# Another table of queue orders for a two-layer diffusion trunk on one Trainium2 core

## The chip, the cores and the metric

The kernel runs on one core of one Trainium2 chip. A core has five instruction queues that run side by side and meet only at semaphores: TensorE (PE, the matmuls; their weight loads are shown apart as PEld), VectorE (DVE), ScalarE (ACT), GpSimd (POOL) and SyncE (SP, which issues most loads). The metric is the device time of one execution in microseconds (us); lower is better.

## What is computed

A diffusion trunk of two layers over 512 latent tokens and 256 context tokens of width 1024, in float32. Every sub-layer stands between two RMS norms, with shift, scale and gate worked out from a conditioning vector (adaLN). Layer 0 mixes tokens by neighbourhood attention beside spatial gating, layer 1 by retention; each is followed by a gated MLP with a depthwise convolution of three taps. Cut to what matters:

```python
def conv_ffn(h, w_in, conv_w, conv_b, w_out):
    a = dwconv3(h @ w_in, conv_w, conv_b)
    gate, up = jnp.split(a, 2, axis=-1)
    return (jax.nn.silu(gate) * up) @ w_out

for i in range(2):
    sh1, sc1, g1, sh2, sc2, g2 = jnp.split(silu(c) @ ada_w[i] + ada_b[i], 6, axis=-1)
    h = modulate(rmsnorm(x, norm_g[i, 0]), sh1, sc1)
    y = hybrid_na_sgu(...) if i == 0 else retention_mixer(...)
    x = x + g1 * rmsnorm(y, norm_g[i, 1])
    h = modulate(rmsnorm(x, norm_g[i, 2]), sh2, sc2)
    x = x + g2 * rmsnorm(conv_ffn(h, ...), norm_g[i, 3])
```

In layer 0 the context tokens go through the same steps, with a conditioning vector of their own.

## The kernel before

**Matmuls.** Tokens are cut into six tiles of 128 rows (t = 0 to 3 latent, 4 and 5 context). A float32 product is made of three fp32r matmuls: each operand x is split into a rounded copy hi (ACT, L171) and the rest lo = x - hi (DVE, L172), and `mm3` issues hi by hi, hi by lo and lo by hi (L216 to L218), all into one PSUM tile. PSUM has three groups of tiles, A (four buffers), B and C (two each). A PE instruction that opens a new PSUM tile waits until the tile before it in that buffer was read out by ACT or DVE.

**The FFN.** The products of the tokens with the two halves of w_in (gate and up) use a two-level Strassen-like scheme: sums of weight blocks (the split tiles wa, wb, wc and wd, built by DVE at L1618 to L1630 and split at L171 and L172) times sums of token blocks (blk, hb, hs; in layer 0 they travel through DRAM on their way, L607 and L622). The results px and py (L215 to L218) are emptied into the tile pre by ACT (L1574) and DVE (L1579); convolution (ACT L1586, DVE L1587 and L1590), Silu (L1593) and product (L1594) give g. In layer 1 the first blocks are made by plain products, pf, with the weights wp. The product with w_out, tile wf, is copied by ACT (L1730) into one of four slots (yp0 twice, ypg twice) and from there added to the rows yd or yf by a DMA with accumulation that POOL issues (L1734).

**Between sub-layers.** The last out-projection of the retention adds its PSUM tiles wrA and wrC to the token tiles yr (DVE L678); then come the square sums (ACT L403), the RMS factors (POOL L408 and L389), gate (DVE L434), residual (DVE L441), a second norm (L453 on DVE for one half of the row, L454 on ACT for the other), transposes on PE (tile ht, L552) and their scaling (ACT L560, DVE L562). In the attention the scores s (L1066, L1067) use keys ka and kb; kb is completed by a cast on POOL (L1021), and the bias tiles tm are made on POOL too (L1049 to L1056); softmaxed rows sc are transposed to pt (L1136) and multiplied with the values (L1144 to L1151). Beside all this runs the adaLN of later sub-layers: DVE accumulates weight rows (L326), PE sums them and turns them by two-column transposes (at, L370) or multiplies them out (ag, L347), and POOL loads the norm gains ngr (L352) and stores the gates (L356).

**What sets the order.** The program text records its instructions first. `Trunk.queue()` then reads the table ORDER: for each of the five engines it gives, as differences, a permutation of the instructions that were recorded for that engine, and `queue()` chains them with dependencies that need no semaphore, so that each engine issues its instructions in the order of the table. What an instruction waits for (data, free buffers) follows from the tiles and is the same in any order.

Of the kernel before, what the change touches and what calls it, by code (L numbers as in the profile page):

```python
# [51 lines left out]
c-p;Nd8{4RS^wtDnSI~x+<kxd?Yp1-{1(SsV#izD_}N+P#Ez4YCUKi4X_Is#ZBx`#Ep3Bn)0P4)sBEQz3Mx<wv>*_mB2>|Tsf0u&{s0Li{@`D}Gt  # L52
0d*cX6Ie%CYaAJ2Pj_obxTe@ArK(PX+)BbckC8n$bRh-#=2s?*@MGjDZ{0)zEWi_4p&YxNS9|21<GeE+yMdm<kKg;1FHHn!XWj=Hk6ia<||U96SM
gxYLERfTJ7&IFfcwwyOXOU;~&_5D$0i9{3c8+s|=Hk3Z)=&Xp_pLvwKOD!l9C9CZ5Er(4@Nyawbd{;D0^#BUOh4HuzeorTj$U$$VJ3^)O9%~&$Y^
gXs$hPS_|L;JJrYh^;`yOQmM^SCNW9Q?+14X)#N6+eglLBE61YPGFbfBsdF$BbhR9n7t}kjjg-dHg&EkH$N9N6SGWUKlfGyVIYPv63!T!*4Nj-{F
h0^JqlNc&nDZ;x!Il=d#i}GSvAIfCuv$Xk{&SzipDXu1`4rKWtK8CAnkg4*o)Rsx;no6MM+EEr1tcbD}YAvF(XeX7@v&$ZUr6R4qD!>ph2?U+18J
oBE^h?c}z-ak`$vB|Q9&PqQv3mYD&$*Wq*>fawyZ``woEv$%$z$0HPo&TJgIy{;Zb3sPgTFSB(y41P{#JEHS5aELB=Z}vnav-s}pg0oO(mKLA80q
|Y!J6!ILpC|FO5O*R$9ecKaYBR5RCZvzDi$4G#W`eqf=vRf8Q33#al-=|V4l#%!%0tN|XP9#&R&@D=;l=Jns9HoYdkWwtJb8QLm6O@vc9AJ(*d!0
+_I^7usKHWk>G0od_dhszlPwu%59|Nf@9-s(S@aX>O0oSu+kS%^Bb58|CcO?{WW9cceQ5~MQDdHr-hVU^-=zpPN1gVavHjuLPJ9`=3mf9uxAf_ZS
YSDsAHa4Tt|9@)&~!HO%IdM$Vg7-G&kp>}Pe%DZ2mi_?qg5m4u_~z-e33KZZ#npD4!)OmVVAx1RJ8cv`LH|7O!u|-JRcn#Mb)Fn;vwcL^RZ(?iS0  # L60
+T(zOV7!W@zhd)M|jxR350iLo`)2k0;xS%Pu6nrUvV1j8LYHIJ&SL^3^*&;)(#5ZR-+!d=+f&I8m--%L$vXTmJ*hT||XrVZMkaPW7@P|v_;2X^|k
{?A|Ih6gwoeLpZ^_?g6#(uVBet}k<MaJv)wA5B;Z{Cq-VATmBtijaCSodQk>H*8wB(kq`FiWLVMj8LtypHF9DV$h12aIijz#Wlu~97wc0A78N%Ay
cC5Z2Wz4oYr2Cr20lywx8qP|1YuZ{yr<h!^4+e0cOZ{Y+6zRc+j_=6a9JTA?x^dN~3bqDGp*Cz<0Rsa&&O+tGHV#{^?*g-{w|NXRghvt(*BB1t-Y
%Je8fvUvQB}=Q>=^=;q!1qfd|3MgGQFgN~P2h`ZXE6P3t$661kM?!1zjecY-!C-W0%v#zvawJ>t?{Cnb98`G!t!8q~vdAv|vg55M`WR^jm%_=|n@
xc+92E!h{njJqY_ow>%Spl7nY_s3$>6P0P986E$a&gE@6PS&^;t5Pe8*5lrXoE*CcSn?WJ*Gc-hLy={4&+F-h1xm?_hs$>J$ZZ4IvGJ^CA6De$v|
2|G^id6a4K`?*dVT~rBV0!0W-cZLM+9Rdv8QtkHSNK#@af=CQLxsSsm+;ebAlBT4Mo@9^R}(1b@JxUrx4bactPhs`>DhN%5u{OFp8tTiX{Oixa|W
M%#LD{6u`uhd<9H`5qqJVo1M`hO1a_>F!xJ`Ga}kB|usl{LY%v-gfMpAA(n53NQW)-sxAlMBeE@sYIIb3@-J<2peo+ae(8y{iK0~zMT;i8ujU&fu
_d7*CVmwx2wsxD<i2`qdpGxo*jp(N0O{8vhnxcJt0pT3A9Bf-}9sCNNly8388;{qr-{aI$k8u?CdYxo2EH#YNfStxZ6n~)J$Q$bs8du0^3`5R-}<
Oi>2YD^44P`K_MRh=Gk1z@xW**bSq0TGHN-4aP%qe!Hj%beI~TCIF!1pG&Q6Rrkm9vF>XYxsmokGVhs;;V?%#GytF|_;Oz3=1c^U4;2gI}R8LLlv
!CQQvCV~q3%ijnk0mBq>4(35W<Q;?)VFBj1S{Q*>Hc);mSal<Lny~i)3{6(nH0VGxVhhXkjbaM&;4a=3wxLG>yNpZYyW^_>C=<XuoExl`agZ=RfG  # L70
d$6!nKWZu?0x_Hd?saPrM=41T_E?9n^ZmXkvQb0~G+cS*(1B_Fwh#1IU=_(Ggtj%!``=^D+kma{Q!g#l<%0al)eBcC3K`-8(M+L=FhG5YbFaVM4}
{{en}Z$w2g2hA)isZ_<_`bu0Q8m%FuH00SkTG>a)N69{*`p&9r`)S1lp5yjv;w=4kK4sx|u1Xpe9^`$fGJ&Ap5D!}ze<gAW#yw7aA)V*rkd`+yEv
}b*gd605%1^i-bMTD2UuYSf`T8r&6?@q@)X5cnCyD1y6`S?)sQv*rQw;eUdE!p>d%=ii;6&OylVc4(3r!w97L&w8OoQ8P)shV04GvG;GwE(u2}<>
KF4Ea843$xNVn0j$Bd(vD-+=HomX@vDEW=wCOnyY*hh#Y6UV)!&D`ps0K8Z!xyXRD5g7>{$@T#Vn2B>>!z4Ssf`aP#$Br_gq@5j#zgN(yMc#LAj(
{XSqkV?PoJW3&wlKFrLPgKdnnKI37qV)P$x>Wh8pA9{e55<^^#I@A{>R-P708b+hy~Yh=>wWN3f@^Awjy?YT%{bEsCa_1c6a1a%_Rq!|{jCY4<VX
GEf5pL<xW%Xn3#`<dOlP*Ami`$x-f4co-3iXc-w*BY68rz)Qy+v^3UA$O*i3ekz?jKQSXdd99WWrAwo)c|=IqJa@X`;%M9y$q_O=)C2|e9C&hnqV
w^~SC`DCTuTmk7V+K=OY|HS13(6t;<j^ge6e!@MUsm1N9O^AeFkMH(nu3sfM2>+k$0*wuDDK@c}B6H7|5cUVL_ndm0_*wOiZF`bqJqvG(ihfp6E-
`cIw&`4c6?=p7b|#l`DsaFU;N!-DJBWNqYc+>XGGezmTpa989%v{uu_$<NU!rs4>WFFE%=zsPxxPYKq?r`)o{FB-jSt6}YEGXiXQ6Es@+IIAB0H$
QUws%Ce_#o$*SI0oJ)A?yZ*j@<Nr30Cvd2K*<<gs0``&bYNIv-^S>yXSUcK=#{Q3l!E5+@^N$XA~4gW?K-1Po)HuK)B<2?a`$L?bwJ`u@G?s@)KI
QEQsj+LwSAdcYye1=PLyp_{yCyl;?h%QGjP|!SX+<bg_nAG87zs-#}Mla7f^Vnm>b>4Sndv1<NM$BQn%2M9q$CA7L4VTM0?j8ladvb*HFpOuxQ|Y  # L80
3vWh+@9<GwXM{B%oM_hVll80=q4$wqUe$cS1v38!o)|Bxsep*(P@d52^SYHHwP)9J`hM1=ZuzpA)5NPN%atueOJ|H>@m>tx7)5&^2(uvL$?42Hzv
`I+SjmFY>1dB=zM0o&J;sUePhlpB=C;6KxytE2QFX7MYvwB+&J;M8x#N4^<V(vT{?6tkL@R1CA31>~Hok*E5R<iFm(=`VBeCda<z^ZCRl70bz3u_
WQ(?@nvL&B$oZoQ-J_!<onNmf28pdCST8=&+cwY0U#e$ai)`jPWwh4LKAm=Kg!OTC|dY?H3q<9v8t7R=kngUi5y*_qY|jzj8v1MYYQ;ovAwZ>dUW
lNvieo1QW?(%F4SY1l-|Aq7TC5VS7yBYh@pmn@k)Ha*?C|#z0b-Kb{}GGc=hkwoJ@X{w?nP&(Y?0xsfaOV0gAG`G++(;^$o~${x>xNwR=PpNv5|G
s1~sv6Q}&z3*$>ZEG|yPoQ{}zQirKG1U(!{WdU;`K*ovoJpoAmwiTY<18}<hSq(kyca%{1?{U@idl=%aA$&nygYJb^vV44SW1AHo=v3|Cl$$W*Sg
93X{Qt84%6u7^b<@soA7n^U8kmTEts&UsHy~XYG!uLk=muT!xWF0f_(fE6@1H-KJ-XSl?)e%KCPk!-+0Uh@5WWB0E(t+s$DB6IL47(q^IH>T@;kf
# [1959 lines left out]
```

## Time and profile before

| | |
| --- | --- |
| time, median of 3 runs | 1784.99 us (1783.62 to 1786.71) |
| time of the profiled execution | 1783.88 us |
| span of the profile | 1782.1 us |
| mean TensorE clock granted | 0.996 |
| HBM read, written | 191.80 MB, 39.85 MB |
| attention (layer 0) | about 190 to 345 us of the span |
| FFN of layer 0 | about 400 to 1040 us |
| FFN of layer 1 | from about 1418 us |

The span is the part of the execution between the first and the last recorded instruction; 1.8 us of the profiled time lie around it. A queue runs in order: an instruction that waits holds up all that stand behind it on its engine, and idle time of an engine costs only where the engine that ends last waits for it.

### The profile page before, as it was taken

What the parts mean: (1) busy time and instruction counts of PE and PEld (TensorE: products, weight loads), DVE (VectorE), ACT (ScalarE), POOL (GpSimd) and SP (SyncE); (2) the same over time, 40 slices, a digit from 0 to 9 for tenths busy, and PEclk for the clock granted to TensorE, in tenths of its full rate; (3) what the DMA queues carried; (4) which work ended last, traced back from release to release, by engine and by line L of the source; (5) the groups of instructions that cost most, each with busy time, mean ns of one, the idle gap of its engine ahead of it and who ended that gap; (6) DMA issues with size and microseconds to landing.
All of it is one profiled execution on the core that took longest, in us unless ns stands there. A gap on an engine that the chain in (4) does not pass through costs nothing.

```text
span 1782.1 us, 28774 instructions
## 1 busy us (share of the span) xinstructions
PE 1746.4 (98%) x11024; PEld 1576.8 (88%) x11024; DVE 1388.4 (78%) x2363; ACT 1017.1 (57%) x1882; POOL 338.9 (19%) x462
## 2 busy tenths in 40 slices
...
GB/s 306 116 133 168 96 109 43 107 180 119 171 178 172 180 172 153 169 172 160 271 112 135 109 120 64 119 98 86 90 72 60 107 126 152 206 220 183 177 148 129
DMA packets 84398, 253.44 MB, mean 142 GB/s; under 512 B 11026, under 2 KB 11538, under 8 KB 84260
## 3 DMA queue, kind: packets, MB, share of 16 engines
...
q14 instruction: 52, 0.43, 0.1%
HBM read 191.80 MB, written 39.85 MB: 130 GB/s over the span
## 4 chain that ended last, share of the span: by engine, by line
PE 89%; DVE 5%; ACT 2%; DMA 1%; issue 1%; POOL 1%; SPq 0%; DVEq 0%; POOLq 0%; ACTq 0%
PE px L215 12%; PE wf L216 5%; PE wf L217 5%; PE wf L218 5%; PE rn L217 4%; PE rn L216 4%; PE rn L218 4%; PE py L215 4%; PE px L218 2%; PE px L216 2%; PE px L217 2%; PE py L218 1%; PE py L217 1%; PE py L216 1%; PE ug L216 1%; PE ug L217 1%
## 5 line engine op out<-in xcount | busy, mean ns | idle before, releaser
L326 DVE SCALAR_TENSOR_TENSOR acc<-ar,cs,acc 128x512 f32<-128x512 f32 x256 | 190.1, 757 | 12.0 <-DMA ar<-in_adaw 5.1
L216 PE MATMUL rn<-rwv,h0c 128*128 128x256 f32 x384 | 107.8, 281 | 0.0
L217 PE MATMUL rn<-rwv,h0c 128*128 128x256 f32 x384 | 107.5, 281 | 0.0
L218 PE MATMUL rn<-rwv,h1c 128*128 128x256 f32 x384 | 107.2, 280 | 0.0
L1734 POOL DMA_DIRECT2D yf<-yp x64 | 55.9, 962 | 265.8 <-ACT yp L1730 238.3
L1574 ACT ACTIVATE pre<-px 128x256 f32<-128x256 f32 (+2 forms) x160 | 55.9, 369 | 78.2 <-PE px L215 56.1
L1587 DVE SCALAR_TENSOR_TENSOR cv<-pre,cw,cv 128x769 f32<-128x769 f32 (+1 forms) x88 | 77.2, 882 | 27.7 <-ACT cv L1586 27.1
L1586 ACT ACTIVATE cv<-pre,cw 128x770 f32<-128x770 f32 (+1 forms) x88 | 80.9, 925 | 21.5 <-DVE g L172 11.6
L1730 ACT COPY yp<-wf 128x512 f32<-128x512 f32 x118 | 68.3, 583 | 42.3 <-PE wf L218 34.4
L215 PE MATMUL px<-blk,wb 128*128 128x384 f32 (+1 forms) x480 | 78.8, 308 | 1.1 <-ACT pre L1574 1.1
L215 PE MATMUL px<-hs,wc 128*128 128x384 f32 (+1 forms) x480 | 78.7, 309 | 1.1 <-ACT pre L1574 0.8
L1590 DVE SCALAR_TENSOR_TENSOR cv<-pre,cw,cv 128x769 f32<-128x769 f32 (+1 forms) x88 | 76.8, 881 | 0.9
L215 PEld LDWEIGHTS px<-hs,wc 128*128 128x128 f32 x480 | 73.2, 188 | 4.2 <-ACT pre L1574 1.6
L215 PEld LDWEIGHTS px<-blk,wb 128*128 128x128 f32 x480 | 72.4, 188 | 3.8 <-ACT pre L1574 1.6
L171 ACT ACTIVATE wc<-q 128x512 fp32r<-128x512 f32 x80 | 49.8, 629 | 43.8 <-PE py L215 21.7
L216 PEld LDWEIGHTS rn<-rwv,h0c 128*128 128x128 f32 x384 | 72.4, 189 | 1.2 <-issue 0.2
L218 PEld LDWEIGHTS rn<-rwv,h1c 128*128 128x128 f32 x384 | 72.5, 189 | 0.7
L217 PEld LDWEIGHTS rn<-rwv,h0c 128*128 128x128 f32 x384 | 72.3, 188 | 0.9
L218 PE MATMUL rn<-rwg,h1c 128*128 128x256 f32 x256 | 71.3, 279 | 0.0
L1734 POOL DMA_DIRECT2D yd<-ypg x48 | 48.3, 1052 | 120.3 <-ACT ypg L1730 102.9
L217 PE MATMUL rn<-rwg,h0c 128*128 128x256 f32 x256 | 71.2, 279 | 0.0
L216 PE MATMUL rn<-rwg,h0c 128*128 128x256 f32 x256 | 71.1, 279 | 0.0
...
## 6 DMA issues: line engine op xcount, KB each, us to landing
...
```

The costliest lines, as they stand in the source:

```text
L171: self.S.activation(hi, src, AF.Copy)
L215: mm = lambda *p, **k: self.T.matmul(*p, skip_group_check=True, **k)
L216: mm(out, lhs[0], rhs[0], start=first, stop=False)
L217: mm(out, lhs[0], rhs[1], start=False, stop=False)
L218: mm(out, lhs[1], rhs[0], start=False, stop=last)
L326: V.scalar_tensor_tensor(out=acc[s], in0=raw[:, kk * 512 : kk * 512 + 512], scalar=self.cs[:, 8 * s + k : 8 * s + k + 1], in1=acc[s], op0= ...
L1574: S.activation(pre[:, i, c : c + w], ps[:, b : b + w], AF.Copy, scale=scale)
L1586: S.activation(d, s, AF.Identity, scale=w1, bias=b)
L1587: V.scalar_tensor_tensor(out=d[:, 1:W], in0=s[:, 0 : W - 1], scalar=w0, in1=d[:, 1:W], op0=ALU.mult, op1=ALU.add)
L1590: V.scalar_tensor_tensor(out=d[:, 0 : W - 1], in0=s[:, 1:W], scalar=w2, in1=d[:, 0 : W - 1], op0=ALU.mult, op1=ALU.add)
L1730: S.copy(v, ps)
L1734: G.dma_start((yd[t] if first else y[t])[:, o], v, accum_op=ALU.add)
```

## The change

Only the string ORDER differs: 72 lines of text become 112. No instruction is added or taken away, tiles and their buffers are the same; one more load of an activation table appears at the start, where ACT's order changes between two functions. The text of the table is compressed, so a line of it tells nothing by itself:

```diff
 LANES = ("PE", "DVE", "Activation", "Pool", "SP")
 ORDER = """
-c-p;Nd8{4RS^wtDnSI~x+<kxd?Yp1-{1(SsV#izD_}N+P#Ez4YCUKi4X_Is#ZBx`#Ep3Bn)0P4)sBEQz3Mx<wv>*_mB2>|Tsf0u&{s0Li{@`D}Gt
...
+c-pmlXLRJ)b>@8l3aJ1TfI{V*t4J1E%sDi3X0w}Qv%AR-(|M-jO!tHilQjyXFr#Eiqd2mHNA_wYTN+zFYiVuo`gqqX$79L)*p`pit6ke`uXoQ```CLgs>
...
```

The table being 40 lines longer, every line number behind it is 40 higher in the new kernel (L216 becomes L256, L1730 becomes L1770).

What it does is seen in the queues. PE's queue is printed with equal neighbours joined: it has 8847 rows before and 9761 now. ACT, in the FFN of layer 0, at block 9 (wc9 and wb9 are its weight sums, yp0 and ypg the slots for w_out's pieces wf). Before:

```order
L1730 COPY ypg_4613<-wf0430_5768 128x512
L1730 COPY ypg_4613<-wf0431_5815 128x512
L1574 ACTIVATE pre00_4125<-px08_5722 128x384
L171 ACTIVATE wc9_5856<-q49_5858 128x512
L171 ACTIVATE wb9_5806<-s29_5807 128x512
L1730 COPY yp0_4612<-wf0641_5874 128x512
L1730 COPY yp0_4612<-wf0640_5865 128x512
L171 ACTIVATE wb9_5806<-s39_5808 128x512
L1586 ACTIVATE cv08_5913<-pre00_4125,cw0_4123 128x770
```

and now:

```order
L1770 COPY ypg_4613<-wf0430_5768 128x512
L1614 ACTIVATE pre00_4125<-px08_5722 128x384
L211 ACTIVATE fo07h_5824<-fo07r_5826 128x1024
L1770 COPY ypg_4613<-wf0431_5815 128x512
L211 ACTIVATE wb9_5806<-s39_5808 128x512
L211 ACTIVATE wb9_5806<-s29_5807 128x512
L1770 COPY yp0_4612<-wf0640_5865 128x512
L1770 COPY yp0_4612<-wf0641_5874 128x512
L1626 ACTIVATE cv08_5913<-pre00_4125,cw0_4123 128x770
```

The copies of wf0640 and wf0641 stood behind the first split of wc9; now they stand ahead of both, which follow four and eleven rows behind.

POOL, some 30 us later in the same FFN (ngr0110 is a load of norm gains for a later sub-layer, yd0 the accumulating stores of token tile 0). Before:

```order
L1734 DMA yd5_4132<-ypg_4613 128x512 x2
L352 DMA ngr0110_6139<-in_norm_g 128x512
L1734 DMA yd0_4127<-yp0_4612 128x512 x2
L317 MEMSET acc100_6209 128x512
L317 MEMSET acc101_6212 128x512
L356 DMA g20_4110<-ngr0110_6139 128x512
```

and now:

```order
L1774 DMA yd5_4132<-ypg_4613 128x512 x2
L1774 DMA yd0_4127<-yp0_4612 128x512 x2
L392 DMA ngr0110_6139<-in_norm_g 128x512
L357 MEMSET acc100_6209 128x512
L392 DMA ngr0111_6205<-in_norm_g 128x512
L1774 DMA yd1_4128<-ypg_4613 128x512
L358 DMA acc100_6209<-in_adab_row 1x16x32
```

The two stores to yd0 have moved ahead of the load; the load ngr0111, which came nine rows after them, now comes ahead of the first store to yd1.

PE, at the end of the retention's out-projection and the start of the FFN of layer 1 (ht12 are the transposes of token tile 2, ht11 and ht10 those of tiles 1 and 0). Before, behind the last matmul of wrC21 stand three transposes, all twelve matmuls of wrC30, one transpose, all of wrC31 and then:

```order
L216 MATMUL wrC31_14642<-rwo71_14460,gt7_14438 128x512
L217 MATMUL wrC31_14642<-rwo71_14460,gt7_14438 128x512
L218 MATMUL wrC31_14642<-rwo71_14460,gt7_14438 128x512
L552 MATMUL ht110_14664<-ident_95,yr01_9944 128x128 x4
L552 MATMUL ht101_14602<-ident_95,yr00_9927 128x128 x4
L552 MATMUL ht111_14673<-ident_95,yr01_9944 128x128 x4
L552 MATMUL ht120_14774<-ident_95,yr02_9961 128x128 x4
L216 MATMUL pf100_14749<-hb1_14475,wp001_14463 128x256
```

Now the last matmul of wrC21 stands in the middle of wrC30:

```order
L258 MATMUL wrC30_14611<-rwo61_14324,gt16_13905 128x512
L256 MATMUL wrC30_14611<-rwo70_14455,gt7_14438 128x512
L592 MATMUL ht100_14593<-ident_95,yr00_9927 128x128
L258 MATMUL wrC21_14571<-rwo71_14460,gt7_14438 128x512
L257 MATMUL wrC30_14611<-rwo70_14455,gt7_14438 128x512
L258 MATMUL wrC30_14611<-rwo70_14455,gt7_14438 128x512
```

and 20 rows behind it:

```order
L258 MATMUL wrC31_14642<-rwo70_14455,gt7_14438 128x512
L256 MATMUL wrC31_14642<-rwo71_14460,gt7_14438 128x512
L592 MATMUL ht110_14664<-ident_95,yr01_9944 128x128
L257 MATMUL wrC31_14642<-rwo71_14460,gt7_14438 128x512
L258 MATMUL wrC31_14642<-rwo71_14460,gt7_14438 128x512
L256 MATMUL pf100_14749<-hb1_14475,wp001_14463 128x256
L256 MATMUL pf110_14790<-hb1_14475,wp101_14692 128x256
L592 MATMUL ht121_14785<-ident_95,yr02_9961 128x128
L592 MATMUL ht120_14774<-ident_95,yr02_9961 128x128
L592 MATMUL ht121_14785<-ident_95,yr02_9961 128x128
```

wrC20, wrC21, wrC30 and wrC31 are woven together, and the transposes of tiles 0 and 1 have moved in among them; ht12 follows right behind.

More of the change, by code (lines that the diff above doesn't have):

```diff
@@ L57 @@
[L57 to L71, printed above, removed]
```

169 lines of the change are left out of this document (112 added, 57 removed).

## The prediction

> **What bounds the kernel.** I read the busy shares first, then the chain of waits that ended last.
>
> ```profile
> span 1782.1 us, 28774 instructions
> PE 1746.4 (98%) x11024; PEld 1576.8 (88%) x11024; DVE 1388.4 (78%) x2363; ACT 1017.1 (57%) x1882; POOL 338.9 (19%) x462
> PE 89%; DVE 5%; ACT 2%; DMA 1%; issue 1%; POOL 1%; SPq 0%; DVEq 0%; POOLq 0%; ACTq 0%
> ```
>
> TensorE (PE) is the bound. The change issues the same matmuls, so it can only touch three things: the time PE waits, the time PE runs at half clock, and what it costs to go from one kind of matmul to another. The view of PE's waits (line, tile, who released it; sum, count, longest) prices the first:
>
> ```profile
> PE ht L1831 <- DVE xn L425: 9.7, 2, 8.0
> PE ht L552 <- ACT sa L560: 3.0, 1, 3.0
> PE wf L216 <- ACT yp L1730: 3.0, 2, 1.7
> PE px L215 <- ACT pre L1574: 1.9, 3, 0.8
> PE pt L1136 <- DVE at L172: 1.4, 3, 0.9
> PE s L1067 <- POOL kb L1021: 1.2, 1, 1.2
> PE wf L216 <- ACT pre L1574: 1.0, 1, 1.0
> PE s L1066 <- DVE sst L1123: 0.9, 1, 0.9
> PE py L215 <- ACT pre L1574: 0.5, 1, 0.5
> ...
> PE rq L216 <- ACT h0c L171: 0.2, 1, 0.2
> ```
>
> The eight largest rows sum to 22.1 us. The next twelve, from the 0.5 to the 0.2 shown, add 3.6. Of these 25.7 us, 9.7 are the start of the kernel, where PE has no data; 16.0 us are left for an order to win. The table by stretches (span, then busy us and count of PE, its weight loads, DVE, ACT and POOL, then clock, DMA share and GB/s) shows where the clock fell:
>
> ```profile
> 190.00:345.00 155.00, 150.20 (x1032) 124.51 (x1031) 122.13 (x344) 105.33 (x262) 36.91 (x51) 1.00 0.26 80
> ...
> 1405.00:1425.00 20.00, 16.18 (x82) 13.32 (x81) 18.09 (x34) 16.52 (x41) 7.62 (x14) 0.95 0.43 159
> 1425.00:1440.00 15.00, 14.62 (x108) 14.32 (x107) 13.99 (x26) 11.50 (x24) 2.15 (x2) 0.84 0.62 216
> 1440.00:1455.00 15.00, 14.40 (x120) 14.00 (x119) 13.26 (x21) 11.51 (x23) 0.00 (x0) 1.00 0.11 37
> 1455.00:1540.00 85.00, 83.28 (x591) 77.46 (x592) 82.50 (x130) 59.32 (x108) 10.41 (x12) 1.00 0.60 162
> ```
>
> At the start of layer 1's FFN the clock averages 0.95 over 20 us and 0.84 over 15 us: 1.0 + 2.4 = 3.4 us lost at most. DVE is the second fact in these rows: from 1405 to 1540 it is busy 18.09 + 13.99 + 13.26 + 82.50 = 127.8 of 135 us. Whatever the order, that stretch cannot shrink by more than about 7 us. The ceiling of the whole change is thus 16.0 + 3.4 us of waits and clock, and about 2 us of kinds of matmul (below): 21 us, 1.2%.
>
> **Places where the new order takes a wait away.** The largest clear one is the w_out product of layer 0's FFN, whose outputs (wf) ACT copies from PSUM to yp. The timeline (start, duration, engine, idle before and its releaser):
>
> ```profile
> 560.48 0.63 ACT L171 ACTIVATE wc<-q 128x512 fp32r<-128x512 f32 x1 [7.82 <-PE py L215]
> ...
> 561.53 1.05 ACT L1730 COPY yp<-wf 128x512 f32<-128x512 f32 x2
> 562.15 0.50 PE L216 MATMUL wf<-fo06h,g 128*128 128x512 f32 x1 [1.71 <-ACT yp L1730]
> ```
>
> ACT's queue stood 7.82 us on the split of wc9, whose buffer PE's py products still read, and the copies that free PSUM stood behind it. In the new order both copies stand ahead of both wc9 splits. PE has matmuls of the next products to run while they copy, so the 1.71 us go; nothing is newly late, since wc9 feeds products of the block after. The second is at 591 us:
>
> ```profile
> 584.73 0.57 POOL L352 DMA_DIRECT2D ngr<-in_norm_g  x1 [12.52 <-DVE wc L172]
> 585.29 1.78 POOL L1734 DMA_DIRECT2D yd<-yp  x2
> 590.93 0.58 ACT L1730 COPY yp<-wf 128x512 f32<-128x512 f32 x1 [2.17 <-DMA yd<-yp]
> 591.57 0.51 PE L216 MATMUL wf<-fo06h,g 128*128 128x512 f32 x1 [1.25 <-ACT yp L1730]
> ```
>
> POOL waited 12.52 us with the load of ngr0110 and kept two yd stores behind it; the yp copy waited for the store to land, and PE for the copy. The new order has the stores first. Behind the load now stand a memset, ngr0111 and the store of yd1, which is not due before the next pair of copies. Gain 1.25 us, and with the first place **-3.0**.
>
> The rows "px <- pre", "wf <- pre" and "py <- pre" (1.9 + 1.0 + 0.5 = 3.4 us) are PE waiting for ACT to empty px: at the starts of the two FFNs and once after the change of product group at 850 us. The new order interleaves the products of two outputs, so that each px has other matmuls behind its last one. I count cover (queued PE work between producer and consumer) that meets the copies at 850 us and at the start of FFN 0, and misses about a third of them after 1440 us, where DVE is at 13.26 of 15 us. Bounds 0 and -3.4; I take **-2.4**.
>
> In attention the rows pt, s and s (1.4 + 1.2 + 0.9 = 3.5 us) are round trips through ACT, DVE and POOL. The POOL cast of kb12 (L1021) now follows tm5 and not tm6, and PE has some four matmuls more ahead of kb12's first use; other scores lose cover. Adding up the missing cover in both orders I get about 4.5 us before and 3.2 now: **-1.3**, between 0 and -2.5.
>
> **A place where it looks worse: the start of FFN 1.** Token tile 2's last out-projection (wrC21) must pass residual, norms and a rescale before its transposes ht12:
>
> ```profile
> 1410.46 0.39 PE L218 MATMUL wrC<-rwo,gt 128*128 128x512 f32 x1
> ...
> 1413.55 0.39 PE L218 MATMUL wrC<-rwo,gt 128*128 128x512 f32 x1
> ...
> 1414.12 0.39 PE L217 MATMUL wrC<-rwo,gt 128*128 128x512 f32 x1
> ...
> 1416.43 0.39 PE L218 MATMUL wrC<-rwo,gt 128*128 128x512 f32 x1
> 1416.66 1.47 PE L552 MATMUL ht<-ident,yr 128*128 128x128 f32 x12
> 1421.17 0.63 PE L552 MATMUL ht<-ident,yr 128*128 128x128 f32 x4 [3.04 <-ACT sa L560]
> ```
>
> From the end of wrC21 (0.23 us after 1410.46, the spacing that 1416.43 and 1416.66 show) to ht12 went 10.5 us. Before, PE had 24 wrC matmuls (0.23 each) and 16 transposes (twelve take 1.47 us and four 0.63, so 0.84 / 8 = 0.105 each) to run: 7.2 us, and it waited 3.04. Now wrC20 to wrC31 are woven together, and behind wrC21's last matmul stand 15 wrC, 10 transposes and two pf of half the width: 4.7 us. If the chain still needs 10.5 us, the wait is 5.8, 2.8 more. But DVE, which sets the chain here (18.09 of 20 us), reaches wp101 after some 2 us less work in the new order, so later waits for it shrink: between -1 and +2.8, I take **+1.0**. I leave the drop of the clock as it is, since it followed a wait of this length and the wait grows.
>
> The Trainium skill, page "TensorE: Matmul & The Clock Gate", section "Why this matters for your kernels", asks for no PE idle gap above about 3 us, as one idle window brings the clock back to half. The trace agrees: 3.04 us of wait, then 0.84. By that rule an order which broke this wait into pieces under 3 us would win the 3.4 us as well, and the sum below would be -8.8; the new order does not break it.
>
> **Kinds of matmul.** Two-column transposes (at, L370) cost extra when they stand among wide products:
>
> ```profile
> 168.86 0.39 PE L218 MATMUL pk<-h0a,wk 128*128 128x512 f32 x1
> 169.18 0.40 PE L370 MATMUL at<-ident,arow 2*128 2x2 f32 x4
> 169.51 0.50 PE L216 MATMUL pv<-h0a,wv 128*128 128x512 f32 x1
> 169.84 0.39 PE L217 MATMUL pv<-h1a,wv 128*128 128x512 f32 x1
> ```
>
> ```profile
> L370 PE MATMUL at<-ident,arow x48: 195/197/219, 169.2 to 1348.4; 2*128 2x2 f32 x48
> ```
>
> From 168.86 to 169.84 are 0.98 us, of which the two wide matmuls are 0.46; the burst of four took 0.52. One lasts 0.197 (the median of 48, second fence) and four last 0.40, so a step is 0.068 and four are 0.27; the other 0.25 are the burst's entry and exit. The order has 19 such bursts before and 15 now: 4 x 0.25 = -1.0. The plain fp32 bursts fall by about three; their entry is at most the same 0.25 (0 to -0.75; I take -0.4). Together **-1.4**. The 128-column transposes are spread over twice as many bursts, at no price: from 1413.55 to 1414.12 stand two wrC (0.46) and between them one transpose alone, which so costs 0.11 us, as one of twelve in a row does.
>
> **The start.** ACT now squares xn04 first and loads the table for Silu after it; SP sends ident ahead of xn05.
>
> ```profile
> 0.72 1.28 ACT L223 ACT_TABLE_LOAD   x1 [0.72 <-PEq L2034]
> 6.69 0.63 ACT L403 ACTIVATE jx<-xn 128x512 bf16<-128x512 f32 x1 [0.62 <-DMA xn<-in_x]
> 10.14 0.90 PE L1831 MATMUL ht<-ident,xn 128*128 128x128 f32 x3 [1.67 <-DVE xn L425]
> 10.97 1.87 PE L266 MATMUL ad<-ar,cs 128*2 128x256 f32 x4
> ```
>
> A second table load of 1.28 us plus Silu less the 0.62 us that ACT idled puts xn05 some 0.75 us later. In exchange a transpose and two ad matmuls (1.87 / 4 = 0.47 each), 1.05 us, stand in PE's wait of 1.67. Bounds -1.05 and +0.75: **-0.3**. The last seventy rows of every queue are as before: 0.
>
> **What the tight order costs.** Counting, for each PE wait, how much queued work covers it, I find 94 covered by less than 0.5 us before and 220 now. The twelve small rows of the waits (3.6 us) over those 94 make 0.04 us each; 126 more make 0 to +4.8. Most of the new ones have more than 0.25 us of cover, so **+2.0**.
>
> The sum is -3.0 - 2.4 - 1.3 + 1.0 - 1.4 - 0.3 + 2.0 = -5.4 us on the profiled run of 1783.88 us (span 1782.1): 1778.5. The profiled run lies 1.1 us under the median of the three runs shown, 1784.99; half of that added, I forecast **1779.0**, 0.3% faster.
>
> **Rivals.** (a) Nearly every wait goes, that at FFN 1 too: 16.0 + 3.4 + 1.4 = 20.8 at most, 12 or more if DVE's 127.8 us in 135 let it: 1764 to 1772. For it speaks that all named waits are touched; against it ht12's cover of 4.7 for 10.5 us. Chance 0.12. (b) The waits change their places: the gain of -7.4 without the last term is eaten by new ones of 4 to 11 us: 1781 to 1788, no change. For it speaks the count 94 to 220. Chance 0.24. (c) Slower: a round trip across engines that the queue covers by under 0.25 us (50 before, 97 now) runs late by its hops. Above, PE started 0.1 us after the yp copy and store after copy cost more. At 0.12 us on each of the 97, 11.6 us, the gain is gone and 0.2% with it; at 0.15, 14.6 us, the time is 1792. Against it: the 50 of before cost at most the 3.6 us of small rows, 0.07 each. Chance 0.12. (d) The half clock comes more often: each drop is worth 3.4 us as at 1405, and three turn the sum to +4.8, 1789. Against it: attention lost 4.8 of 155 us in short waits at a clock of 1.00. Chance 0.04. The same page of the Trainium skill, in "A second HAM failure mode: psum-queue depth-cycling", tells of this: frequent short idles at PSUM buffers made the clock swing; the row of attention speaks against it here. That the table does nothing can be excluded: every queue differs from it by the order of rows.
>
> **Chances and range.** My forecast, between -3.6 and -12 us, has 0.48. Faster still is (a), 0.12; no change is (b); the slower side is (c) and (d), 0.16. A change under 0.2%, 3.6 us, can hardly be told from none here. Faster 0.60, same 0.24, slower 0.16. The range from 1766 to 1791 takes in the bounds of the terms (-3.4, -2.5, +2.8, +4.8) and most of (a) and (b).
>
> **What would show it.** Right: no 1.7 us row for wf, a POOL queue whose yd stores come before ngr, px rows under 1.5 us together, ht12 waiting 3 to 5 us with the clock at half after it, and some 4 to 6 us of waits of 0.1 to 0.4 us. Wrong: a stretch outside 1405 to 1455 below a clock of 1.00, a new wait above 2 us, or no wait at ht12.

## The result, and the profile after

The changed kernel takes **1775.99 us** (median of 5 runs, 1775.4 to 1776.8), against 1784.99 before: the ratio is 0.995, with a 95% interval of 0.9936 to 0.9965. The forecast was 1779.0, in a range of 1766 to 1791. The profiled execution took 1775.40 us, with a span of 1773.6; before they were 1783.88 and 1782.1, so 8.5 us went. The page's head and the shares of the chain that ended last:

```profile
span 1773.6 us, 28862 instructions
PE 1747.3 (99%) x11024; PEld 1570.8 (89%) x11024; DVE 1394.7 (79%) x2363; ACT 1025.0 (58%) x1883; POOL 344.5 (19%) x462
PE 47%; DVE 1%; POOL 1%; ACT 1%; issue 0%; DVEq 0%; POOLq 0%; ACTq 0%
```

PE's busy time is the same within 1 us, with the same 11024 matmul rows. The span shrank, so what went is time in which PE stood: span less busy time was 35.7 us before and is 26.3 now. (The chain's shares cannot be compared with those of before: the listed ones sum to 50% here and to 99% before.) PE's waits of the changed kernel (line, tile, releaser; sum, count, longest; the lines lie 40 further down, since the table is longer):

```profile
PE ht L1871 <- DVE xn L465: 7.8, 1, 7.8
PE pf L256 <- ACT hb L211: 2.6, 1, 2.6
PE pf L256 <- ACT wp L211: 1.3, 1, 1.3
PE rkc L258 <- DVE rwk L212: 0.7, 1, 0.7
PE px L255 <- ACT pre L1614: 0.6, 2, 0.4
...
PE py L255 <- ACT pre L1614: 0.4, 1, 0.4
PE pf L258 <- DVE wp L212: 0.4, 1, 0.4
PE rn L258 <- DVE h1c L212: 0.4, 1, 0.4
...
PE htc L527 <- DVE hc L538: 0.3, 1, 0.3
PE pt L1176 <- DVE sst L1163: 0.3, 1, 0.3
```

Of the rows of before, both for "wf <- yp" (3.0 us) and the one for "wf <- pre" (1.0) are gone, px and py wait 1.0 instead of 2.4, the second wait for xn is gone, and the three rows for pt and s in attention (3.5) have shrunk to one of 0.3 for pt. New are the row of 2.6 for pf, in place of 3.0 for ht at the same spot, 1.3 behind it, three at the start of the retention (rkc, rn, htc), and four of 0.3 to 0.5 us that are left out above; two of these, of 0.4 and 0.3 us, lie in attention. By stretches (span, then busy us and count of PE, weight loads, DVE, ACT and POOL; clock, DMA share, GB/s):

```profile
190.00:345.00 155.00, 153.64 (x1045) 127.68 (x1045) 125.81 (x349) 107.11 (x266) 37.97 (x53) 1.00 0.27 80
1415.00:1430.00 15.00, 12.92 (x86) 11.93 (x87) 13.78 (x26) 13.64 (x29) 4.71 (x6) 0.77 0.56 179
1430.00:1445.00 15.00, 15.00 (x129) 15.00 (x129) 15.00 (x25) 9.43 (x18) 0.00 (x0) 1.00 0.03 7
```

```profile
1415.35:1422.10 6.75, 5.02 (x19) 4.03 (x20) 5.53 (x10) 5.67 (x13) 4.10 (x6) 0.50 0.22 86
```

In attention PE is busy 153.64 of the same 155 us, 150.20 before, so it stands for 1.36 us and not for 4.80. At the start of FFN 1 the clock falls again, to 0.77 over 15 us; the last row shows that it is at half from the end of the wait of 2.55 us on, for 6.8 us.

To see **where** the time went I use rows of PE's queue ahead of which the very same matmuls stand in both orders, and take the difference of the times at which PE reaches them. Between two such rows the work is equal, so a change of the difference belongs to that stretch:

| stretch of the profile before, us | forecast for what lies in it | measured |
| --- | --- | --- |
| start, to 86 | -0.3 | -1.6 |
| 86 to 215, products ahead of attention | part of the tight order | +0.6 |
| 215 to 337, attention | -1.3 | -3.05 |
| 337 to 410, start of FFN 0 | part of -2.4 (px, wf, py <- pre) | -1.0 |
| 410 to 598, the two places with yp and yd | -3.0 | -3.05 |
| 598 to 857, change of product group | part of -2.4 | -0.9 |
| 857 to 907, end of FFN 0, start of retention | part of the tight order | **+2.2** |
| 907 to 1398, retention | part of the tight order | +0.85 |
| 1398 to 1467, start of FFN 1 | +1.0, and part of -2.4 | -1.6 |
| 1467 to the end | nothing | -1.0 |

Kinds of matmul (-1.4) are spread over the stretches. The measured column sums to -8.5.

### The profile page after: what moved, and what is told of

Its sections match the earlier page's. It is cut to its first block, busy times and chain, and to the rows that moved or that the text cites. A ratio compares the mean times of both kernels' runs of the same rounds, so it can differ in the third digit from the quotient of the medians.

```text
span 1773.6 us, 28862 instructions
## 1 busy us (share of the span) xinstructions
PE 1747.3 (99%) x11024; PEld 1570.8 (89%) x11024; DVE 1394.7 (79%) x2363; ACT 1025.0 (58%) x1883; POOL 344.5 (19%) x462
## 4 chain that ended last, share of the span: by engine, by line
PE 47%; DVE 1%; POOL 1%; ACT 1%; issue 0%; DVEq 0%; POOLq 0%; ACTq 0%
PE px L255 5%; PE rn L258 4%; PE rn L256 4%; PE rn L257 4%; PE wf L256 2%; PE wf L257 2%; PE wf L258 2%; PE py L255 2%; PE wr L258 1%; PE wr L257 1%; PE wr L256 1%; PE rk L257 1%; PE rk L256 1%; PE rk L258 1%; PE rq L258 1%; PE rq L257 1%
## 5 line engine op out<-in xcount | busy, mean ns | idle before, releaser
L255 PE MATMUL px<-hs,wc 128*128 128x384 f32 (+1 forms) x480 | 108.4, 308 | 0.2 <-ACT pre L1614 0.2
L256 PE MATMUL rn<-rwv,h0c 128*128 128x256 f32 x384 | 106.6, 282 | 0.0
L257 PE MATMUL rn<-rwv,h0c 128*128 128x256 f32 x384 | 104.8, 280 | 0.0
L255 PE MATMUL px<-blk,wb 128*128 128x384 f32 (+1 forms) x480 | 103.3, 308 | 0.4 <-ACT pre L1614 0.4
L1770 ACT COPY yp<-wf 128x512 f32<-128x512 f32 x118 | 68.6, 583 | 51.6 <-PE wf L258 47.0
L255 PEld LDWEIGHTS px<-hs,wc 128*128 128x128 f32 x480 | 80.8, 188 | 5.7 <-ACT pre L1614 0.5
L255 PEld LDWEIGHTS px<-blk,wb 128*128 128x128 f32 x480 | 79.2, 188 | 5.1 <-ACT pre L1614 1.0
L256 PEld LDWEIGHTS rn<-rwv,h0c 128*128 128x128 f32 x384 | 71.9, 188 | 2.1
L1774 POOL DMA_DIRECT2D yd<-yp x48 | 45.4, 973 | 135.2 <-ACT yp L1770 123.6
L255 PE MATMUL px<-hs,wd 128*128 128x384 f32 x240 | 69.9, 338 | 0.0
L256 PE MATMUL rn<-rwg,h0c 128*128 128x256 f32 x256 | 69.7, 279 | 0.0
```

What stands on the lines that cost most here:

```text
L255: mm = lambda *p, **k: self.T.matmul(*p, skip_group_check=True, **k)
L256: mm(out, lhs[0], rhs[0], start=first, stop=False)
L257: mm(out, lhs[0], rhs[1], start=False, stop=False)
L1770: S.copy(v, ps)
L1774: G.dma_start((yd[t] if first else y[t])[:, o], v, accum_op=ALU.add)
```

## Experiments

Twelve kernels, each an order of the same instructions unless said otherwise. "Local" means the difference at rows of PE with the same matmuls ahead, in the profiles of the kernels named. In the diffs the rows of a queue stand without line numbers.

| kernel | time, us (runs) | before, same chip | ratio, 95% interval |
| --- | --- | --- | --- |
| before, copies first | 1783.48 (10) | 1784.39 | 0.9992, 0.9983 to 1.0001 |
| before, stores first | 1783.19 (10) | 1784.39 | 0.9995, 0.9986 to 1.0004 |
| before, new order to 86 us | 1782.12 (10) | 1784.16 | 0.9991, 0.9981 to 1.0000 |
| before, new order to 337 us | 1779.37 (10) | 1784.16 | 0.9975, 0.9966 to 0.9985 |
| changed, FFN 1's start in the old order | 1777.43 (4) | 1784.39 | 0.9959, 0.9944 to 0.9974 |
| changed, PE kept busy | 1776.22 (4) | 1784.16 | 0.9958, 0.9943 to 0.9973 |
| changed, PE kept busy, wp101 first | 1777.53 (4) | 1784.34 | 0.9961, 0.9946 to 0.9976 |
| changed, pf100 and wp101 first | 1777.96 (4) | 1784.34 | 0.9962, 0.9947 to 0.9977 |
| changed, retention's start in the old order | 1776.52 (4) | 1784.39 | 0.9954, 0.9937 to 0.9970 |
| changed, two rows of DVE earlier | 1778.98 (9) | 1784.16 | 0.9966, 0.9956 to 0.9976 |
| changed, PE alone old from 848 to 900 us | 1776.63 (4) | 1784.34 | 0.9954, 0.9938 to 0.9971 |
| changed, PE alone old from 877 to 900 us | 1776.41 (5) | 1784.46 | 0.9957, 0.9943 to 0.9971 |

None beats the changed kernel's 1775.99, and the intervals of the last eight overlap that of the changed kernel (0.9936 to 0.9965). Single terms of 1 to 2 us are near what total times can tell, so the readings rest on the local differences of one profile of each kernel.

### The two places of yp and yd, one at a time

Copies first, on ACT, and stores first, on POOL, each as a change of the kernel before:

```diff
 ACTIVATE pre00_4125<-px08_5722 128x384
+COPY yp0_4612<-wf0641_5874 128x512
+COPY yp0_4612<-wf0640_5865 128x512
 ACTIVATE wc9_5856<-q49_5858 128x512
 ACTIVATE wb9_5806<-s29_5807 128x512
-COPY yp0_4612<-wf0641_5874 128x512
-COPY yp0_4612<-wf0640_5865 128x512
```

> The kernel before, with one change on ACT alone: the copies of wf0640 and wf0641 to yp stand just ahead of the first split of wc9. Theory: this alone is what the new order wins at 552 to 562 us. The wait of 1.71 us of PE for the yp copy goes, PE runs on, and the rest of the span is shifted by it: 1.7 us less than before, no row of 1.7 for wf in PE's waits. Rival: wc9 is now later and its reader waits, or the store of yp decides; then PE waits elsewhere within the next 10 us and the time is that of before within 0.5 us.

```diff
 DMA yd5_4132<-ypg_4613 128x512 x2
+DMA yd0_4127<-yp0_4612 128x512 x2
 DMA ngr0110_6139<-in_norm_g 128x512
-DMA yd0_4127<-yp0_4612 128x512 x2
```

> The kernel before, with one change on POOL alone: the two stores to yd0 stand ahead of the load of ngr0110. Theory: the yp copy at 591 us no longer waits for a store to land, the 1.25 us of PE go, and the time is 1.2 us less; the row wf <- yp keeps only its 1.7. Rival: the store lands late for another reason (the DMA queue is full of weights), and PE still waits about 1 us there: no change.

The waits of more than 1 us for wf that each has left, first with the copies first, then with the stores first (timeline: start, duration; idle before and releaser):

```profile
592.01 0.50 PE L213 MATMUL wf<-fo06h,g 128*128 128x512 f32 x1 [1.52 <-ACT yp L1727]
```

```profile
564.14 0.50 PE L213 MATMUL wf<-fo06h,g 128*128 128x512 f32 x1 [1.71 <-ACT yp L1727]
```

Each edit takes away its own wait (1.71 and 1.25 before) and leaves the other. Locally the first wins 1.3 us and the second 1.5. The 1.3 is less than 1.71 because a new wait of 0.38 stands at 567.88, for the copy to ypg; and the first gives back 0.3 at 592, where the other wait is now 1.52 and not 1.25. The two sum to 2.8, and the whole change wins 3.05 there: two separate mechanisms, each as forecast. The total times (-0.9 and -1.2 us, with intervals that reach 1) agree with that but would not show it alone.

### Start and attention: are the parts independent?

Before with the new order of all five queues up to 86 us, and in a second kernel up to 337 us, the old order behind it. The first rows of PE show the idea of the start: four rows that need only xn04 or ar stand ahead of the first that needs xn05.

```diff
 MATMUL ht020_168<-ident_95,xn04_89 128x128
+MATMUL ht021_174<-ident_95,xn04_89 128x128
+MATMUL ad00_160<-ar000_161,cs_93 2x256 x2
 MATMUL ht020_168<-ident_95,xn05_91 128x128
```

> The kernel before, with the new order of all queues for the first 86 us alone. My prediction gave the start 0.3 us, counting two ad matmuls of 0.47 us in PE's wait for xn05. The profile of the changed kernel shows four such rows there, 1.87 us, so the whole wait of 1.67 is filled. Theory: the start wins 1.2 to 1.9 us, 1782.5 to 1783.2. Rival: xn05 comes 0.65 later and the rest is the scatter of the first loads; the gain is under 0.5 us.

> The kernel before, with the new order of all queues for the first 337 us (start and attention) and the old one behind. Theory: the gains are local and add up; the two profiles give 1.2 us for the start and 3.05 us for the attention, and the runs so far show the start of the kernel before 0.7 to 1.4 us later still, so 4.3 to 5.5 us less than before: 1779 to 1780. My prediction's terms were 0.3 and 1.3: 1782.8. Rival: the gain of the attention only moves a wait into the next stage, 1784.

PE's first rows in the changed kernel show how the wait of 1.67 us of before is filled:

```profile
7.82 0.69 PE L1871 MATMUL ht<-ident,xn 128*128 128x128 f32 x2 [7.82 <-DVE xn L465]
8.60 1.86 PE L306 MATMUL ad<-ar,cs 128*2 128x256 f32 x4
```

The two ad00 matmuls appear as four rows of 0.47 us, 1.86 us in all, and no wait stands behind them. With the new order up to 86 us, the profile wins only 0.3 to 0.6 us locally, since ad waited 1.3 us for ACT's jx there. The start scatters from run to run: the same row of PE was reached at 88.0 to 89.8 us in the three profiles with the old start and at 85.8 to 88.2 in the eleven with the new one, means 89.1 and 87.0. The total times of this kernel also differ by 2.0 us (1782.12 against 1784.16). So the start is worth about -2.0 us; the -1.6 of a single pair of profiles is not exact.

With the new order up to 337 us the local win is 4.3 us at 337, 3.5 at 900 and 4.5 at the end, and the total time is 4.8 us less: what is gained there is not eaten by a later stage. The stretch of 155 us shows it alone (same kernel):

```profile
190.00:345.00 155.00, 153.14 (x1043) 127.33 (x1042) 125.78 (x348) 107.60 (x268) 38.99 (x54) 1.00 0.28 82
```

Idle times of PE above 0.18 us sum to 4.5 us in this stretch before and to 1.0 in the changed kernel.

### The start of FFN 1

In the changed kernel PE's rows there are these:

```profile
1412.41 0.40 PE L258 MATMUL wrC<-rwo,gt 128*128 128x512 f32 x1
...
1415.36 0.58 PE L256 MATMUL pf<-hb,wp 128*128 128x256 f32 x1 [2.55 <-ACT hb L211]
...
1417.26 0.58 PE L256 MATMUL pf<-hb,wp 128*128 128x256 f32 x1 [1.32 <-ACT wp L211]
1417.88 0.90 PE L592 MATMUL ht<-ident,yr 128*128 128x128 f32 x3
```

A first kernel puts this stretch (1392 to 1460 us, all queues) back into the old order, where the out-projections run one after the other and the transposes of tiles 0 and 1 in rows behind them:

```diff
-MATMUL wrC20_14552<-rwo60_14319,gt06_13904 128x512
-MATMUL wrC21_14571<-rwo60_14319,gt06_13904 128x512
...
+MATMUL wrC20_14552<-rwo60_14319,gt06_13904 128x512
+MATMUL wrC20_14552<-rwo60_14319,gt06_13904 128x512
```

> The changed kernel, with all five queues in the old order between 1392 and 1460 us (last out-projections, start of layer 1's FFN). My prediction made this place 1.0 us worse in the new order and gave a gain of about 1.0 to the waits that follow until 1460; in the two profiles the stretch took 1.6 us less. Theory from the profiles: the old order costs 1.6 us here, 1777.6. Theory of the prediction: the two cancel, 1776 within 0.5. A wait of 3 us at ht12 is expected back in either case, and the clock at half for 6 to 7 us as in both.

PE's waits in it, the first rows behind the start's:

```profile
PE ht L590 <- DVE yr L491: 3.1, 1, 3.1
PE wf L254 <- ACT pre L1612: 1.0, 1, 1.0
PE pf L254 <- ACT hb L209: 0.8, 1, 0.8
```

The local loss is 1.5 us, but not at ht12: the row of pf110 that waits for DVE's half of wp101 starts at 1421.00, against 1421.07 in the changed kernel, which had come to the stretch 0.4 us earlier. The waits have other names there and about the same end. The loss comes at 1447 to 1456 us, where the row for "wf <- pre" is back: four waits of 0.36, 0.48, 0.99 and 0.47 us, 2.3 in all. The new order has two there, 0.8 in all:

```profile
1448.93 0.63 PE L255 MATMUL py<-hb,wc 128*128 128x256 f32 x3 [0.41 <-ACT pre L1614]
1454.84 0.39 PE L255 MATMUL px<-blk,wb 128*128 128x256 f32 x1 [0.36 <-ACT pre L1614]
```

The second kernel asks what the half clock costs. 34 transposes of token tile 0 (yr00) stand in the waits, 24 ahead of the first pf100 and 10 ahead of the first pf110; their results are overwritten.

```diff
+MATMUL ht120_14774<-ident_95,yr00_9927 128x128 x24
 MATMUL pf100_14749<-hb1_14475,wp001_14463 128x256
+MATMUL ht120_14774<-ident_95,yr00_9927 128x128 x10
 MATMUL pf110_14790<-hb1_14475,wp101_14692 128x256
```

> The changed kernel, with 34 more transposes on PE whose results are overwritten: 24 ahead of the first pf product, 10 ahead of the second, in the two waits of 2.55 and 1.32 us at the start of layer 1's FFN. They add about 3.6 us of PE work that fits into these waits. Theory: the waits let the clock fall to half for some 7 us; with PE busy the clock stays at 1.00 and the products that now run at half speed run at full speed, so that up to 3.4 us are won, less what DVE holds up: 1772.5 to 1774. Rival: DVE and ACT set the pace here until 1423, so that the products wait for them as long as they ran slowly: the clock stays up, but less than 0.5 us is won. Second rival: transposes do not count as activity and the clock falls all the same.

The same stretch, and PE's largest wait behind the start's:

```profile
1415.00:1430.00 15.00, 12.72 (x105) 11.98 (x104) 13.78 (x26) 13.56 (x30) 4.83 (x6) 1.00 0.55 173
```

```profile
PE pf L258 <- DVE wp L212: 1.6, 1, 1.6
```

The clock stays at 1.00, and nothing is won: PE gets to the next row sooner and waits there 1.6 us for DVE's half of wp101. Local difference at 1482 us: 0.0 (+0.26 ahead of the stretch, +0.22 behind it). DVE is busy 13.78 of 15 us both times.

So the next two put DVE's wp101 ahead of a residual, the third kernel with the added transposes, the fourth without them and with the six pf100 and the ht12 ahead of the first pf110 on PE:

```diff
 TENSOR_TENSOR yr03_9978<-yr03_9978,G110_9052 128x512
+TENSOR_TENSOR wp101_14692<-wp101r_14693,wp101_14692 128x1024
 SCALAR_TENSOR_TENSOR xd3_14625<-yr03_9978,yd3r_14662,xd3_14625 128x512 x2
-TENSOR_TENSOR wp101_14692<-wp101r_14693,wp101_14692 128x1024
```

> The kernel with PE kept busy at the start of layer 1's FFN, and DVE's lower part of wp101 moved ahead of the two residual rows of xd3, where DVE idles 0.76 us for POOL. With PE kept busy the clock stayed at 1.00 and nothing was won, since PE then waited 1.6 us for wp101 from DVE until 1421. Theory: with wp101 first that wait goes and the full clock pays: 1.2 to 1.8 us less at 1425 than with PE kept busy alone, 1774.5. Rival: the residual of the last token tile is the chain that counts, it comes 0.5 to 1.2 us later, and PE waits for its transposes ht13 instead: no gain or 0.5 us more.

```diff
 MATMUL pf100_14749<-hb1_14475,wp001_14463 128x256
+MATMUL pf100_14749<-hb1_14475,wp001_14463 128x256 x5
+MATMUL ht120_14774<-ident_95,yr02_9961 128x128 x4
+MATMUL ht121_14785<-ident_95,yr02_9961 128x128 x4
 MATMUL pf110_14790<-hb1_14475,wp101_14692 128x256
```

> The changed kernel, with six products of pf100 and then the eight transposes of ht12 ahead of the first pf110 on PE, and DVE's wp101 ahead of the residual rows of xd3 as in the run beside it; no added work on PE. Theory: the wait of 1.3 us for wp101's upper part (1415 to 1417 us) is filled with pf100, and the pf110 rows find wp101 ready: 1.0 to 1.5 us less than the changed kernel at 1425 us, with the clock still at half for some 7 us. Rival: DVE's other rows (hb, the residual of the last tile) set the time of ht13 and of the later pf rows, and the gain is under 0.4 us.

The wait for hb that appears 7 us later in each, first in the third kernel, then in the fourth:

```profile
1422.79 0.38 PE L257 MATMUL pf<-hb,wp 128*128 128x256 f32 x1 [2.11 <-ACT hb L212]
```

```profile
1422.64 0.38 PE L257 MATMUL pf<-hb,wp 128*128 128x256 f32 x1 [1.91 <-ACT hb L212]
```

At 1421.66 both are 1.4 us ahead of the changed kernel, at 1426 they are 2.7 and 2.4 behind; before the stretch it was +0.8 and +0.6. Both thus lose 1.8 to 1.9 us, in two steps. The 1.22 us of DVE that were moved forward stand in front of the residual that norm, yr and hb follow from. The wait for hb is where they show: behind it both are where they were before the stretch (+0.7 and +0.6), and a row for DVE's part of hb adds 0.4. The other 1.5 and 1.4 us come in the next 3.4 us, in which PE does not wait and the clock is at half, first in the third kernel, then in the fourth:

```profile
1424.00:1427.30 3.30, 3.30 (x18) 3.30 (x17) 3.30 (x7) 2.66 (x5) 0.00 (x0) 0.50 0.58 173
```

```profile
1423.80:1427.10 3.30, 3.30 (x18) 3.30 (x16) 3.30 (x7) 2.71 (x5) 0.00 (x0) 0.50 0.43 170
```

In the changed kernel the half clock is over at 1422.1, and until 1421 PE waited for DVE and ACT anyway. Two more profiles fit this. The kernel with the retention's start in the old order has the changed kernel's order here and half clock for 3.4 us, over at 1420.6; it wins nothing by that. The kernel with two rows of DVE earlier (below) has this order too, but half clock from 1420.2 to 1430.5, and loses 1.9 us. So the chain through DVE and ACT sets this start until about 1422; PE's order and clock do not matter up to that time; behind it the clock does.

### The new loss at the start of the retention

PE's new waits in the changed kernel, and what DVE does around them:

```profile
885.86 0.39 PE L258 MATMUL rn<-rwv,h1c 128*128 128x256 f32 x1 [0.36 <-DVE h1c L212]
887.05 0.52 PE L527 MATMUL htc<-ident,fin 128*128 128x128 f32 x3 [0.25 <-DVE hc L538]
893.75 0.39 PE L258 MATMUL rkc<-h0c,rwk 128*128 128x256 f32 x1 [0.65 <-DVE rwk L212]
```

```profile
891.14 1.42 DVE L481 SCALAR_TENSOR_TENSOR fin<-yf,yc3r,fin 128x512 f32<-128x512 f32 x2 [0.84 <-POOL yc3r L429]
892.48 1.22 DVE L212 TENSOR_TENSOR rwk<-rwk0r,rwk 128x1024 fp32r<-128x1024 f32 x1
```

DVE stands 0.84 us for a norm from POOL, with the split of rwk0 behind it. Four kernels ask what brought this about. The first puts all queues back into the old order from 848 to 900 us; on DVE, for instance:

```diff
+TENSOR_TENSOR rwv00_8674<-rwv00r_8675,rwv00_8674 128x1024
 SCALAR_TENSOR_TENSOR cv021_8574<-pre00_4125,cw0_4123,cv021_8574 128x769 x2
 SCALAR_TENSOR_TENSOR cv021_8574<-pre00_4125,cw0_4123,cv021_8574 128x769 x2
+TENSOR_TENSOR cv021_8574<-cv021_8574 128x770
 SCALAR_TENSOR_TENSOR ab10_111<-at13_8603,ng_99 128x4 x2
-TENSOR_TENSOR cv021_8574<-cv021_8574 128x770
-TENSOR_TENSOR rwv00_8674<-rwv00r_8675,rwv00_8674 128x1024
```

> The changed kernel, with all five queues in the old order between 848 and 900 us (end of layer 0's FFN, start of the retention). In the two profiles this stretch took 2.2 us longer in the new order, with waits of 0.4, 0.3 and 0.7 us for DVE. Theory: the loss is local, the new order covers DVE's results too shortly there; the old order in this stretch takes 2.2 us off the changed kernel, some 1773.8. Rival: the old order was good there only because it arrived later, so that DVE and the weights were further ahead; then DVE is late again and less than 0.7 us is won.

Its only gap above 0.18 us from 840 to 900 us:

```profile
856.23 0.47 PE L256 MATMUL wf0A<-fo018h,g 128*128 128x512 f32 x1 [0.95 <-DVE ab L417]
```

The waits at 885 to 894 go, and 1.0 of the 2.2 us comes back. The rest is this wait for DVE at 856, which the old order did not have when it also ran ahead of 848. When ab ran, before, in this kernel, and a wait of DVE in the changed kernel ahead of it:

```profile
862.29 0.22 DVE L377 SCALAR_TENSOR_TENSOR ab<-at,ng 128x4 f32<-128x4 f32 x2
```

```profile
855.86 0.22 DVE L417 SCALAR_TENSOR_TENSOR ab<-at,ng 128x4 f32<-128x4 f32 x2
```

```profile
848.19 0.69 DVE L212 TENSOR_TENSOR al<-acc,ah 128x512 fp32r<-128x512 f32 x1 [1.08 <-ACT ah L211]
```

PE's rows from 857 to 863 of before run 7.8 us earlier here; ab is only 6.4 us earlier. DVE thus comes to this stretch 1.4 us later against PE than before. In the changed kernel and in this one it idled 1.08 us for ACT's ah just ahead of it (at 848.19 and 849.33); before, the same row ran at 856.26 and did not wait. In the changed kernel too DVE is late: it is through with the same rows, up to the split of rwv01, 7.7 us earlier than before, where PE is 8.9 us earlier.

The second moves two DVE rows of the changed kernel ahead of the residuals in front of them, h1c and the split of rwk0:

```diff
 TENSOR_TENSOR yf03_8612<-yf03_8612,fin_8610 128x512 x2
+TENSOR_TENSOR rwk0_9013<-rwk0r_9014,rwk0_9013 128x1024
 SCALAR_TENSOR_TENSOR fin_8610<-yf03_8612,yc3r_9004,fin_8610 128x512 x2
-TENSOR_TENSOR rwk0_9013<-rwk0r_9014,rwk0_9013 128x1024
```

> The changed kernel, with two moves on DVE alone at the start of the retention: the lower part of h1c from hc21 stands ahead of the two residual rows of xtg, and the lower part of rwk0 ahead of the two residual rows of fin (DVE idles 0.84 us there for POOL). The run with the old order in this stretch took away the three waits for DVE at 885 to 893 us, but brought a new one of 1.1 us at 856 of its own making, so 1.0 us was won at 900 us and the total did not show it. Theory: DVE's order alone makes the waits; both moves take 0.5 and 0.8 us away and the retention begins 1.0 to 1.3 us earlier, 1774.9. Rival: the residuals that are now later delay the next token tile, PE waits at its transposes or at hc instead, and the start of the heads (rk0) comes at 900.4 as before, within 0.3.

```profile
PE htc L528 <- ACT hc L537: 1.8, 1, 1.8
```

This row of PE's waits is new. The residual that was pushed back feeds the norm of the next token tile, and its transposes htc and hc come late. Locally 2.3 us are lost between 885 and 899 us. Up to 894 the moved rows win 1.3 us; the wait takes these and 0.6 more; and 1.6 us are lost in the 3.4 us behind it, at half clock:

```profile
896.84 0.33 PE L528 MATMUL htc<-ident,yf 128*128 128x128 f32 x1 [1.85 <-ACT hc L537]
```

```profile
898.00:901.30 3.30, 3.30 (x18) 3.30 (x17) 2.48 (x4) 2.38 (x5) 0.00 (x0) 0.50 0.39 160
```

The theory fell. The rival names the place of the new wait, for hc, but not the size: rk0 comes 2.3 us later, and not within 0.3. The profile is the slowest of the nine runs of this kernel, which scatter from 1775.59 to 1781.28.

The third and fourth put PE alone back, from 848 and from 877 us on. In the fourth, for example:

```diff
-MATMUL rn02_9104<-rwv00_8674,h0c_8691 128x256
-MATMUL htc23_8938<-ident_95,fin_8610 128x128
-MATMUL htc01_9033<-ident_95,fin_8610 128x128
-MATMUL htc00_9006<-ident_95,fin_8610 128x128
+MATMUL htc23_8938<-ident_95,fin_8610 128x128 x2
 MATMUL wf0C31_8984<-fo018h_8623,g0118_8067 128x512
```

> The changed kernel, with PE alone in the old order between 848 and 900 us; DVE, ACT, POOL and SP as changed. Theory: the loss of 2.1 us there comes from PE's order, which runs the last products of layer 0's FFN (wf0C) early and has little left beside the first products of the retention while DVE and ACT finish the token tiles; with the old order on PE the waits for DVE at 885 to 893 go and rk0 starts at 898.2 to 898.8 instead of 900.4, counted from the same start of the stretch. Rival: DVE and ACT are themselves later in the new order; PE in the old order then waits for them at other tiles, and rk0 starts within 0.5 us of 900.4.

> The changed kernel, with TensorE alone in the order of before, and only for the rows from 877.4 to 900.2 us of the changed kernel's profile (the last transposes htc of FFN 0's output and the first retention matmuls rn, rkc, rk); the rows ahead of it and the other four queues keep the new order. Theory (the matmuls rn and rkc stand too early in the new order of TensorE's own queue, and the wait at 856 us of the two runs before came only from putting the earlier rows back too): the waits of 0.36, 0.25 and 0.65 us at 885 to 894 us fall to under 0.7 in sum, no gap over 0.5 us appears near 856 us, and the rows at 900 us come 0.7 to 1.5 us earlier against the rows at 840 us than in the changed kernel; the total 1774.5 to 1775.5 us. Rival (VectorE's operands h1c, hc and rwk end when they end, and TensorE's order only decides which matmul stands waiting for them): the same sum of waits within 0.4 us at other rows between 885 and 897 us, and the total 1775.5 to 1776.8 us.

The gaps above 0.2 us from 850 to 900 us, of the third and then of the fourth:

```profile
858.87 0.50 PE L258 MATMUL wf0A<-fo,g 128*128 128x512 f32 x1 [0.63 <-DVE g L212]
895.22 0.38 PE L258 MATMUL rkc<-h0c,rwk 128*128 128x256 f32 x1 [0.48 <-DVE rwk L212]
```

```profile
885.56 0.41 PE L528 MATMUL htc<-ident,fin 128*128 128x128 f32 x2 [0.71 <-DVE hc L539]
892.26 0.39 PE L259 MATMUL rkc<-h0c,rwk 128*128 128x256 f32 x1 [0.57 <-DVE rwk L213]
```

They sum to 1.11 and 1.28 us; in the changed kernel it was 0.36 + 0.25 + 0.65 = 1.26. Locally the third wins 0.7 us and the fourth 0.15. As to the waits, PE's order mostly chooses which matmul stands waiting; what it waits for ends when DVE gets to it. The waits are not the whole loss: 0.9 of the 2.2 us lie in the spacing of matmuls outside of them, and some 0.5 of these came back with the old order on PE from 848 us on. That DVE comes late to the stretch is shown (1.4 us against PE); that its 1.08 us of idling for ah, which the new order put ahead of the split of rwv00, is the cause fits in size, but was not tried apart and stays open.

## Why the prediction was right, and where it was off

The direction and the kind of gain were right: waits of PE went, and the work did not change. The size was short, -5.4 forecast and -8.5 measured between the two profiles, and that the sum is not further off is partly luck: terms that were too small (attention, the start) and gains that were not forecast stand against a tight order that cost more. By its steps:

- **yp copies and yd stores (-3.0): right.** -3.05 in the whole, and -1.3 and -1.5 apart. ACT's and POOL's queues each held a short row behind one that waited.
- **px, wf and py waiting for pre (-2.4): right.** By the rows of waits the 3.4 us became 1.0, and "misses about a third of them after 1440" fits too: there 0.51 + 1.00 + 0.47 became 0.41 + 0.36. The three stretches show more, -1.0, -0.9 and -1.6, since other things lie in them: a wait of 0.33 for DVE's wb went as well, the rest was not traced.
- **Attention (-1.3): right in kind, less than half in size.** The mis-sized term is the 3.2 us of missing cover in the new order. Before, PE's idle times above 0.18 us sum to the 4.5 that were counted; now they sum to 1.0. Measured -3.05, beyond the bound of -2.5, and -2.4 with the +0.6 ahead of it.
- **Start of FFN 1 (+1.0): wrong.** Of the -1.6 there 1.5 are the waits after 1440, so the start itself cost nothing. The chain was right: 10.4 us from the end of wrC21 (1407.5) to ht12 (1417.9). The step that failed was the price of less cover on PE. The rows in between took 6.5 us and not the 4.7 that were counted, two pf at half clock among them, so the wait of 3.04 did not grow to 5.8; it was replaced by 2.55 for hb and 1.32 for wp in front of ht12, because DVE and ACT set the time of all of them. The forecast had noted that DVE sets the chain and yet counted cover on PE.
- **The clock (0): right.** It fell again, as forecast, for 6.8 us. But the 3.4 us that were held as "lost at most" were not there to be won in the new order: at a clock of 1.00 the stretch took as long. The Trainium skill, page "TensorE: Matmul & The Clock Gate", section "Why this matters for your kernels", names an idle gap of about 3 us as what brings half rate; here the clock was at half from the end of a wait of 2.55 us, so the limit was lower here. The new order did break the wait of 3.04 into pieces under 3 us, and the clock fell all the same.
- **Kinds of matmul (-1.4): not shown.** No run tried it alone, and PE's busy time did not fall (1746.4 before, 1747.3 now).
- **The start (-0.3): wrong in size.** The working gave two ad matmuls two rows of 0.47 each; they are four, 1.86 us, more than the wait of 1.67 that they fill. Worth about -2.0.
- **The tight order (+2.0): right in kind, wrong in shape.** +0.6, +2.2 and +0.85 make 3.7 us. More than half of it lies in one place, the start of the retention, that the forecast did not name, and not in 126 small covers.

-1.0 us behind 1467 us was not forecast and not traced. Of the signs given for right, no 1.7 us row for wf and px rows under 1.5 us came (px and py at 1.0). The small waits sum to 4.6 us, but some of them are of 0.5 to 0.7 and not 0.1 to 0.4. ht12 itself did not wait, though 3.9 us of waits stand ahead of it with the clock at half. So "no wait at ht12" for wrong came too, as did a new wait above 2 us, that for hb.

Of the rivals, the waits that change places are real (+2.2 at the retention, and FFN 1's start) but ate 3.7 us of some 12. The slower side, 0.12 us on each of 97 short round trips, did not come: outside of waits the spacing of matmuls grew by some 2 to 4 us in all, not by 11.6.
